# The low part of a weight block: one half by a VectorE subtraction, the other by an accumulating transfer

## The chip, the cores and the metric

The kernel runs on one core of a Trainium2 chip. The metric is the device time of one execution in microseconds (us); a lower one is better. The engines are named as in the profile: PE is TensorE's matrix products and PEld its weight loads, DVE is VectorE, ACT is ScalarE, POOL is GpSimd, SP is SyncE, which issues most of the transfers.

## What is computed

The reference runs a sequence of 512 tokens of width 1024 through three layers and computes everything in float32. The first layer has pooling beside latent attention, the second has differential attention, and each is followed by a gated feed-forward of width 2816. The third layer mixes three kinds of heads (a stick-breaking attention, a gated recurrence and an attention over 256 memory rows) and ends in a routed block: for each token and each of 8 heads, the 16 best of 16384 experts are chosen and weighted.

```python
def swiglu(h, w_gate, w_up, w_down):
    return (jax.nn.silu(h @ w_gate) * (h @ w_up)) @ w_down
...
h = rms_norm(x, norm_mix_gain[l])
proj = h @ w_in[l]
...
x = x + mixed @ w_out[l]
x = x + peer_ffn(rms_norm(x, norm_ffn_gain[l]), peer_w_query[l], ...)
```

## The kernel before, in words

Every product with a weight matrix is made in split form. A weight w is split into a high part, which is w rounded to the faster matrix type (FR in the code), and a low part, which is w minus the high part. The activations are split in the same way. A product is then three matrix products: high by high, high by low and low by high (`mm3`, L265 to L268; `tok_mm`, L278 to L286, is the same with the tokens as the stationary side, at L283 to L285).

`load_w` (L244) brings in one block of weights, mostly 256 columns of a 1024-row matrix, which is 128 x 2048 numbers or 1 MB. It does so in two halves of 128 x 1024. For each half SyncE loads the numbers into a `raw` buffer (L253), ScalarE copies them into `whi` with rounding (L228), and an engine given by the list LO subtracts `whi` from `raw` into `wlo` (L229). `raw`, `whi` and `wlo` have three buffers each (RB and WB, L32), which is one and a half blocks. With 256 tokens a block means 48 matrix products of 256 columns.

Which engine subtracts is set for a stretch of the program by `low(n)` (L240):

```python
LO = [V, V]
def low(n):
    LO[:] = [GP] * n + [V] * (2 - n)
```

So with n = 2 GpSimd makes both halves, with n = 1 GpSimd makes the first and VectorE the second, and with n = 0 VectorE makes both. The stretches are:

- LO_Q = 2 (set at L886): the second layer's attention, with its query, key and value projections and the first part of its output projection; 17 blocks. `low(0)` at L893 ends it.
- LO_A = 0 (L952): the second layer's feed-forward for the first 256 tokens (`ffn1(0)`).
- LO_Y = 2 (L1354): the memory's projections and the third layer's projections for the first 256 tokens (`memory`, `projections`), with the feed-forward of the other 256 tokens (`ffn_b`) begun beside them.
- LO_M = 2 (L1357): the mixer of the first half with `ffn_b` beside it, its output projection (`HA.output`), the norm, and the routing queries of that half (`PA.queries`) with `ffn_b` beside them. LO_Y and LO_M hold 56 blocks together.
- LO_Z = 1 (L1724): the rest of `ffn_b`, the projections of the second half, its mixer and its output projection; 22 blocks.
- LO_P = 1 (L1743): the queries of the second half and the expert scores; 72 blocks.

The order of the work has two sources. `alongside` and `side_by_side` (L152 to L182) interleave generators by given step counts, for example `alongside((mixer(HA), 200), (ffn_b, F_2))` at L1359. The order on each engine is then laid out at build time by the tile framework's planner (`schedule_with_timeline_sim=True`, L1799), which knows the dependences and its own estimates of durations; on the chip each engine runs its list in order. `tc.high_priority` draws the small steps of a reciprocal root forward (`rsqrt`, L288 to L300: eleven VectorE steps on a few columns, one after another).

GpSimd also makes some sums of squares (L366, L945), the masks and running sums of the stick-breaking attention (L1252, L1263, L1266), memsets, and it issues the gathers of expert rows (L1516), which are kept in program order. In the routing (`route` and `decode`, L1449 to L1512) VectorE finds the best 16 of the scores; its steps with two operands in SBUF are the candidate sums (L1479) and the one-hot products (L1501, L1504). On SyncE stand the weight loads, one behind another.

## Time and profile before

| what | value |
|---|---|
| median of 3 runs | 3099.04 us (3092.49 to 3104.55) |
| profiled execution | 3092.14 us |
| its span, first to last instruction | 3090.4 us |
| mean granted clock of TensorE | 0.977 |
| busy share: TensorE, its weight loads, VectorE, ScalarE, GpSimd | 95%, 82%, 70%, 44%, 38% |
| the chain that ended last: TensorE, VectorE, transfers | 71%, 18%, 5% |
| moved by SyncE's queue, by GpSimd's queue | 427.61 MB, 137.71 MB |

The table shows one execution in the small, and the runs in its first line. A busy share is an average over stages with different limits, so it says little about what one stage waits for; the views by stage do that. TensorE's products are pipelined: a product's own duration is longer than the time from one to the next. The granted clock is TensorE's, as a share of the full 2.4 GHz. An engine's idle time is counted in front of the instruction that ends it, with what released that instruction. The transfers that GpSimd issues are nearly all gathers of expert rows, and they begin, but for one, after 1800 us.

### The profile page before, as it was taken

What the parts mean: (1) busy time and instruction counts of PE and PEld (TensorE: products, weight loads), DVE (VectorE), ACT (ScalarE), POOL (GpSimd) and SP (SyncE); (2) the same over time, 40 slices, a digit from 0 to 9 for tenths busy, and PEclk for the clock granted to TensorE, in tenths of its full rate; (3) what the DMA queues carried; (4) which work ended last, traced back from release to release, by engine and by line L of the source; (5) the groups of instructions that cost most, each with busy time, mean ns of one, the idle gap of its engine ahead of it and who ended that gap; (6) DMA issues with size and microseconds to landing.
All of it is one profiled execution on the core that took longest, in us unless ns stands there. A gap on an engine that the chain in (4) does not pass through costs nothing.

```text
span 3090.4 us, 44585 instructions
## 1 busy us (share of the span) xinstructions
PE 2923.3 (95%) x16770; PEld 2539.4 (82%) x16770; DVE 2154.9 (70%) x3873; ACT 1370.7 (44%) x2347; POOL 1163.8 (38%) x722
## 2 busy tenths in 40 slices
PE   8999999999989979999879989889999999999999
PEld 6468888877679978789878588889999998777887
DVE  6755434477766755757986658999778758888753
ACT  4443222366544544554344543336656643333332
POOL 3110000243330177466654136555545535445200
PEclk9999999999999999999999989999999999999999
DMA  3012232321145534244443057777888789999964
GB/s 131 28 62 103 86 107 85 104 69 42 28 144 195 181 130 142 77 150 150 135 138 119 1 176 278 258 269 260 292 307 293 286 300 390 369 377 377 342 228 147
DMA packets 195881, 568.29 MB, mean 184 GB/s; under 512 B 16944, under 2 KB 68528, under 8 KB 194000
## 3 DMA queue, kind: packets, MB, share of 16 engines
q1 hardware_dynamic: 157664, 427.61, 40.1%
q0 software_dynamic: 37712, 137.71, 11.9%
q8 instruction: 132, 2.16, 0.3%
q14 instruction: 85, 0.70, 0.1%
q10 hardware_dynamic: 288, 0.11, 0.0%
HBM read 512.93 MB, written 52.43 MB: 183 GB/s over the span
## 4 chain that ended last, share of the span: by engine, by line
PE 71%; DVE 18%; DMA 5%; issue 3%; ACT 2%; POOL 1%; SPq 0%; DVEq 0%; ACTq 0%; POOLq 0%
PE ps L266 14%; PE ps L268 14%; PE ps L267 14%; PE ps L1682 4%; PE ps L1683 4%; PE ps L1681 4%; DVE wlo L229 2%; PE ps L1563 2%; DVE u L1530 2%; PE ps L482 2%; DMA u<-in_peer_v_dram,ix 1%; DMA u<-in_peer_u_dram,ix 1%; PE ps L475 1%; PE ps L283 1%; PE ps L285 1%
## 5 line engine op out<-in xcount | busy, mean ns | idle before, releaser
L229 POOL TENSOR_TENSOR wlo<-raw,whi 128x1024 fp32r<-128x1024 f32 (+2 forms) x240 | 595.7, 2490 | 584.8 <-ACT whi L228 571.0
L228 ACT ACTIVATE whi<-raw 128x1024 fp32r<-128x1024 f32 (+2 forms) x518 | 516.2, 998 | 644.3 <-PE ps L267 367.3
L229 DVE TENSOR_TENSOR wlo<-raw,whi 128x1024 fp32r<-128x1024 f32 (+3 forms) x278 | 351.0, 1264 | 215.3 <-ACT whi L228 214.6
L268 PE MATMUL ps<-yh,wlo 128*128 128x384 f32 (+1 forms) x1152 | 387.0, 337 | 29.4 <-DVE wlo L229 29.3
L266 PE MATMUL ps<-yh,whi 128*128 128x384 f32 (+1 forms) x1152 | 390.8, 339 | 0.0
L267 PE MATMUL ps<-yl,whi 128*128 128x384 f32 (+1 forms) x1152 | 385.4, 335 | 0.0
L1682 PE MATMUL ps<-vl,gh 128*128 128x512 f32 x768 | 300.6, 391 | 5.4 <-DVE vl L229 5.2
L1683 PE MATMUL ps<-vh,gl 128*128 128x512 f32 x768 | 299.3, 390 | 0.0
L266 PE MATMUL ps<-XH,whi 128*128 128x512 f32 (+1 forms) x680 | 273.1, 406 | 8.7 <-ACT whi L228 8.7
L1516 POOL DMA_INDIRECT u<-in_peer_v_dram,ix x128 | 203.2, 1587 | 195.6 <-DVE h L1595 174.2
L267 PE MATMUL ps<-XL,whi 128*128 128x512 f32 (+1 forms) x680 | 267.6, 396 | 0.0
L268 PE MATMUL ps<-XH,wlo 128*128 128x512 f32 (+1 forms) x680 | 263.0, 395 | 1.9 <-DVE wlo L229 1.9
L268 PEld LDWEIGHTS ps<-yh,wlo 128*128 128x128 f32 x1152 | 220.6, 192 | 34.3 <-DVE wlo L229 34.2
L1681 PE MATMUL ps<-vh,gh 128*128 128x512 f32 x768 | 239.5, 392 | 9.2 <-ACT vh L228 9.2
L228 ACT ACTIVATE vh<-raw 128x1024 fp32r<-128x1024 f32 x128 | 133.3, 1055 | 250.0 <-DMA raw<-in_peer_v_dram 174.4
L1530 DVE SCALAR_TENSOR_TENSOR u<-u,h 128x1024 f32<-128x1024 f32 x127 | 190.1, 1502 | 49.3 <-DMA u<-in_peer_u_dram,ix 49.3
L267 PEld LDWEIGHTS ps<-yl,whi 128*128 128x128 f32 x1152 | 221.0, 192 | 0.0
L266 PEld LDWEIGHTS ps<-yh,whi 128*128 128x128 f32 x1152 | 220.9, 192 | 0.0
L366 POOL TENSOR_TENSOR sqa<-sqa,sq 128x512 f32<-128x512 f32 (+1 forms) x28 | 40.8, 1456 | 450.3 <-ACT sq L364 449.4
L266 PE MATMUL ps<-fx,whi 128*128 128x256 f32 x704 | 199.2, 287 | 4.5 <-ACT whi L228 3.1
L268 PE MATMUL ps<-fx,wlo 128*128 128x256 f32 x704 | 193.9, 284 | 6.9 <-DVE wlo L229 4.6
L229 DVE TENSOR_TENSOR vl<-raw,vh 128x1024 fp32r<-128x1024 f32 x128 | 155.0, 1221 | 63.2 <-ACT vh L228 62.7
(427 smaller groups left out, 7146.8 us busy)
## 6 DMA issues: line engine op xcount, KB each, us to landing
raw<-in_uT_dram SPq DMA_DIRECT2D x128, 512.0 KB, 5.8
raw<-in_peer_v_dram SPq DMA_DIRECT2D x128, 512.0 KB, 7.0
raw<-in_w_gate_dram SPq DMA_DIRECT2D x66, 512.0 KB, 3.7
raw<-in_w_up_dram SPq DMA_DIRECT2D x66, 512.0 KB, 3.7
raw<-in_w_in_dram SPq DMA_DIRECT2D x52, 512.0 KB, 3.8
Sd<-s SPq DMA_DIRECT2D x32, 768.0 KB, 7.0
Gd<-st SPq DMA_DIRECT2D x12, 2048.0 KB, 10.4
gt<-Gd SPq DMA_DIRECT2D x32, 768.0 KB, 8.7
```

Source lines behind the costliest of these rows:

```text
L228: SC.activation(hi, src, AF.Copy)
L229: eng.tensor_sub(lo, src, hi.bitcast(F))
L266: PE.matmul(out, wh, xh, start=first, stop=False)
L267: PE.matmul(out, wh, xl, start=False, stop=False)
L268: PE.matmul(out, wl, xh, start=False, stop=last)
L482: PE.matmul(po[hd], vtile(hd, j), t[hd, j], start=j == 0, stop=j == nk - 1)
L1516: i = GP.indirect_dma_start(out=u, out_offset=None, in_=A[table], in_offset=bass.IndirectOffsetOnAxis(ap=self.idx[t, hd][:, j:j + 1], axis=0))
L1530: V.scalar_tensor_tensor(u, u, 1.0, self.h2[t], op0=OP.mult, op1=OP.mult, accum_out=self.sd[t][:, hd, j:j + 1])
L1563: PE.matmul(p[:, n * 128:(n + 1) * 128], q[:, n], e[:, n], start=True, stop=True)
L1681: PE.matmul(p, gh[:, e, ts], h[:, cs], start=False, stop=False, skip_group_check=True)
L1682: PE.matmul(p, gh[:, e, ts], l[:, cs], start=False, stop=False, skip_group_check=True)
L1683: PE.matmul(p, gl[:, e, ts], h[:, cs], start=False, stop=end, skip_group_check=True)
```

## The change

Where LO names the new marker ADDED for a half, the low part is no longer subtracted by an engine. ScalarE makes the high part as before, and then writes minus the high part into `wlo`. GpSimd then issues a transfer that reads the same weights from HBM once more and adds them to what stands in `wlo`. The half's `raw` buffer is needed for the high part alone.

`low(n, other)` now gives the first 2 - n halves to VectorE and the last n to `other`, which is GpSimd where nothing is said. So the order of the halves is turned wherever n = 1. LO_Q, LO_Y and LO_M go from 2 to 1, and with LO_Z (1 as before) they name ADDED: in these stretches VectorE subtracts the first half and a transfer makes the second. LO_P keeps n = 1 with GpSimd, but VectorE now has the first half and GpSimd the second. LO_A is as it was.

```diff
--- before.py
+++ after.py
@@ -31,7 +31,7 @@
 LOWEST = -3.0e38
 RB, WB = 3, 3
 U2, UZ, UD = 3, 3, 4
-LO_A, LO_Y, LO_M, LO_Z, LO_P = 0, 2, 2, 1, 1
+LO_A, LO_Y, LO_M, LO_Z, LO_P = 0, 1, 1, 1, 1
 VB = 4
 HI, HX = 100, 1
 K_S = 8
@@ -43,7 +43,7 @@
 V_0, D_0, N_0, T_0 = 1, 0, 2, 6
 PX, EVX, XX = 1, 0, 1
 Y_F = 0, 4, 0, 0
-LO_Q = 2
+LO_Q = 1
 AT = 2, 6
 E_B = 8, 3
 GB, SB = 1, 1
@@ -237,9 +237,11 @@
         MIXING = [False]
         LO = [V, V]
 
-        def low(n):
-
-            LO[:] = [GP] * n + [V] * (2 - n)
+        ADDED = object()
+
+        def low(n, other=GP):
+
+            LO[:] = [V] * (2 - n) + [other] * n
 
         def load_w(ap, kt, eng=LO):
 
@@ -253,7 +255,12 @@
                 nc.sync.dma_start(raw, ap[:, a * w:b * w])
                 hi = wp.tile([128, 1024], FR, name="whi", bufs=WB)[:, :c]
                 lo = wp.tile([128, 1024], FR, name="wlo", bufs=WB)[:, :c]
-                split(hi, lo, raw, eng[i])
+                if eng[i] is ADDED:
+                    SC.activation(hi, raw, AF.Copy)
+                    SC.activation(lo, hi.bitcast(F), AF.Copy, scale=-1.0)
+                    GP.dma_start(lo, ap[:, a * w:b * w], accum_op=OP.add)
+                else:
+                    split(hi, lo, raw, eng[i])
                 parts.append((hi, lo))
 
             def get(k):
@@ -883,7 +890,7 @@
                 assert scaled[-1] >= 6
                 yield from out_half(A["w_dout"], XH, XL, 1, held, N_0)
 
-            low(LO_Q)
+            low(LO_Q, ADDED)
             for _ in qk(0):
                 pass
             held, scaled = [], []
@@ -1351,10 +1358,10 @@
             yield from steps(h.items(), {H_B[0]: [lambda: between_roots(h.q0)], H_B[1]: [lambda: between_rows(h.q0)]})
             between_inner(h.q0)
 
-        low(LO_Y)
+        low(LO_Y, ADDED)
         alongside((chain(memory(), projections(HA)), 24), (ffn_b, F_1))
         open_mix()
-        low(LO_M)
+        low(LO_M, ADDED)
         MIXING[0] = True
         alongside((mixer(HA), 200), (ffn_b, F_2))
         MIXING[0] = False
@@ -1721,7 +1728,7 @@
 
         alongside((normed(0, W, xh, xl), 20), (ffn_b, F_3))
         alongside((PA.queries(), 112), (ffn_b, F_4), (gather_a, L_4))
-        low(LO_Z)
+        low(LO_Z, ADDED)
         for _ in ffn_b:
             pass
         HB = Half(W, big)
```

## Rows read from the trace of the kernel before

**Rows 1.** busy time, share of the span and instructions of each engine.
```profile
PE 2923.3 (95%) x16770; PEld 2539.4 (82%) x16770; DVE 2154.9 (70%) x3873; ACT 1370.7 (44%) x2347; POOL 1163.8 (38%) x722
```

**Rows 2.** by stage: us, busy us (instructions) per engine, granted clock, DMA share, GB/s.
```profile
607.00:890.00 283.00, 278.96 (x1318) 204.21 (x1318) 198.85 (x472) 160.18 (x310) 110.60 (x71) 0.99 0.20 65
1055.00:1200.00 145.00, 126.03 (x1030) 124.42 (x1028) 75.10 (x142) 71.53 (x115) 101.85 (x65) 0.95 0.45 150
1200.00:1345.00 145.00, 132.34 (x941) 116.34 (x937) 108.51 (x291) 73.20 (x129) 73.82 (x58) 0.94 0.26 90
1345.00:1400.00 55.00, 47.86 (x361) 45.97 (x362) 28.63 (x63) 24.60 (x42) 33.45 (x14) 0.88 0.45 152
1450.00:1595.00 145.00, 117.81 (x916) 113.80 (x915) 142.62 (x409) 58.51 (x98) 93.25 (x47) 0.93 0.43 141
1595.00:1670.00 75.00, 71.92 (x596) 70.88 (x595) 44.99 (x83) 36.37 (x51) 34.08 (x22) 0.97 0.51 174
1800.00:2100.00 300.00, 265.53 (x1584) 260.42 (x1585) 269.62 (x645) 107.48 (x181) 171.41 (x96) 0.94 0.71 247
```

**Rows 3.** groups by shape: busy us, mean ns; last row of 890 to 1055.
```profile
L229 POOL TENSOR_TENSOR wlo<-raw,whi 128x1024 fp32r<-128x1024 f32 x224 | 571.1, 2558 | 550.9 <-ACT whi L228 537.2 <-PE ps L1563 7.1 <-DVE wlo L229 5.7
...
L228 ACT ACTIVATE whi<-raw 128x1024 fp32r<-128x1024 f32 x428 | 451.5, 1056 | 495.9 <-PE ps L267 246.3 <-DMA raw<-in_uT_dram 66.9 <-issue 46.0
...
L229 DVE TENSOR_TENSOR wlo<-raw,whi 128x1024 fp32r<-128x1024 f32 x56 | 69.4, 1243 | 38.7 <-ACT whi L228 38.7
```

**Rows 4.** timeline from 1091.2 us: start us, us, engine, line, operation.
```profile
1091.28 2.38 POOL L229 TENSOR_TENSOR wlo<-raw,whi 128x1024 fp32r<-128x1024 f32 x1
1091.37 2.31 DVE L299 TENSOR_TENSOR rs_c<-rs_c,rs_y 128x2 f32<-128x2 f32 x1
...
1097.37 0.16 DVE L300 SCALAR_TENSOR_TENSOR rcol<-rs_c,rs_y 128x2 f32<-128x2 f32 x1
```

**Rows 5.** chain of waits, 1055 to 1200, then 1200 to 1345: start us, us.
```profile
1088.36 2.29 DVE rs_y L300
...
1125.44 2.22 DVE rs_c L298
...
1200.91 2.40 DVE hg_ks L1186
...
1295.45 2.36 DVE hg_qs L1182
```

**Rows 6.** VectorE groups of 1450 to 1595; then their lines, ns min/median/max.
```profile
L1479 DVE TENSOR_TENSOR cand<-ts 128x256 f32<-128x256 f32 x12 | 14.2, 1179 | 0.0
L1501 DVE TENSOR_TENSOR oh<-af,iota 128x1024 f32<-128x1024 f32 x8 | 13.1, 1642 | 0.0
...
L1499 DVE CAST af<-ai 128x64 f32<-128x64 int32 x8 | 10.0, 1250 | 0.0
...
L1479 DVE TENSOR_TENSOR cand<-ts x32: 398/809/2342, 1426.2 to 2083.9; 128x256 f32<-128x256 f32 x32
L1501 DVE TENSOR_TENSOR oh<-af,iota x16: 1198/1213/3405, 1478.4 to 2126.2; 128x1024 f32<-128x1024 f32 x16
L1499 DVE CAST af<-ai x16: 166/183/2390, 1475.6 to 2116.7; 128x64 f32<-128x64 int32 x16
```

**Rows 7.** GpSimd's plain loads: KB, us to landing; then one issue's ns.
```profile
m<-in_memT_dram POOLq DMA_DIRECT2D x1, 1024.0 KB, 8.8
...
mraw<-in_masks_dram POOLq DMA_DIRECT2D x1, 512.0 KB, 5.9
...
L1007 POOL DMA_DIRECT2D mraw<-in_masks_dram x1: 536/536/536, 871.2 to 871.2; - x1
```

**Rows 8.** busy us and instructions on low parts (wlo), 1450 to 1595.
```profile
1450.00:1595.00 145.00, 80.18 (x288) 55.00 (x287) 9.36 (x7) 78.62 (x32) 0.93 0.43 141
```

**Rows 9.** TensorE's waits, 1055 to 1600, then 1800 to 2100: us, times, longest.
```profile
PE ps L268 <- POOL wlo L229: 7.8, 7, 1.9
...
PE ps L268 <- DVE wlo L229: 29.3, 18, 3.6
```

## The prediction

> **What bounds the kernel now.** I read the page's busy times first [rows 1]: TensorE is busy 95% of the span, so only time in which it stands idle, or runs at the lower clock, can be won. Then the busy times by stage [rows 2], where the reader sees that the idle time is not spread evenly. In the stage of the memory and first projections (1055 to 1200 us) TensorE is busy 126.0 of 145 us, in the first mixer 132.3 of 145, in its output and the norm after it 47.9 of 55, in the query stage (1450 to 1595) 117.8 of 145: 19.0, 12.7, 7.1 and 27.2 us idle. In the query stage VectorE is busy 142.6 of 145 us, so there VectorE is the bound. In the second half's queries (1800 to 2100) TensorE idles 34.5 us.
>
> Next I asked what makes VectorE late. The groups by shape [rows 3] show that a subtraction of 128x1024 takes 2558 ns on GpSimd and 1243 on VectorE where GpSimd makes none. The timeline [rows 4] shows them against each other: a VectorE step on two columns, 0.16 us when alone, took 2.31 us, and it ended with the GpSimd subtraction that had begun 0.09 us before it. The chain of waits [rows 5] passes through seven such pieces in the projection stage (first and last shown, 1.88 to 2.32 us, 15.5 us in all) and nine in the first mixer. In the query stage the same shapes hold VectorE [rows 6]: the candidate sum takes 1179 ns in the mean and 398 at least, the index cast 1250 against 166, the one-hot 1642 against 1198.
>
> **The change, part by part.** From the code: 17 loads of weights are made under LO_Q, 56 under LO_Y and LO_M, 22 under LO_Z, 72 under LO_P; each has two halves.
>
> Removed: GpSimd's subtractions, 34 under LO_Q, 112 under LO_Y and LO_M and 22 under LO_Z, 168 of the 240 on the page; 72 under LO_P stay. The GpSimd time itself is worth nothing (38% busy); what counts is that VectorE is no longer held.
> - Projection stage: seven pieces, 15.5 us, less 7 x 0.16 of their own: 14 us, on a path for which TensorE waits, and under its 19.0 us of idle. I take -14. Ends: 0, if the subtractions that VectorE takes over stand in the same places; -19, all the idle time.
> - First mixer and its output: nine pieces of 1.8 us or more, some 20 us over their own time, but idle is 12.7 + 7.1, and VectorE takes 20 subtractions more (40 halves were GpSimd's, half of them) at 1.2 us, 24 us, in a stage in which it is busy 108.5 of 145. I take -9. Ends: +4 and -20.
> - Query stage: 12 x (1179 - 398) + 8 x (1250 - 166) + 8 x (1642 - 1198) = 9.4 + 8.7 + 3.6 = 21.7 us that VectorE gets back. It pays: 39 halves are made here, 32 by GpSimd and 7 by VectorE [rows 8]; afterwards VectorE has 19.5, so 12.5 more at 1.2, 15 us. That alone leaves -7; other steps with two operands are held too, and I put them at a further -6: -13, since VectorE is the bound here. Ends: +15 and -27 (TensorE's idle).
> - Clock: the granted clock is 0.93 to 0.95 in the three long stages and 0.88 in the output, worth 7, 9, 10 and 7 us; it falls where TensorE has stood idle. With less than half of the idle gone I take -7; ends 0 and -15.
>
> Added on ScalarE: 95 copies that make minus the high part, 1056 ns each by the like-shaped copy [rows 3], 0.1 ms over some 1000 us in which ScalarE is about half busy [rows 2]. They lie beside TensorE; what waits behind one is the next half's high part and the evacuations. Cost 0, within +10; below nothing is excluded, as ScalarE gives no work away.
>
> Added on GpSimd's queue: 95 issues. A plain issue there occupies it 0.54 us [rows 7]; each now waits for the ScalarE copy as the subtraction waited for the high part. Behind it stand the mixer's masks and sums (L1252, L1263, L1266) and, at the very start of the last part, one gather; they had 2.4 us in front of them and now have 0.5. Cost 0, ends -2 and +5.
>
> Added latency, the dear part: after its buffer is free, a second half was ready after a high part and a GpSimd subtraction, 1.06 + 2.4 = 3.5 us. Now it takes 1.06 + 1.06 + 0.54 + the landing. The nearest row is the plain GpSimd load of 512 KB: 5.9 us to landing; the one of 1024 KB took 8.8 [rows 7]. So 8.6 us (11.5 if an accumulation moves twice the bytes), 5.1 us more. Three buffers hold one and a half loads. A load is 48 matrix products at 75 us / 596, 0.126 us: 6.0 us where nothing else runs (36 loads: 2 + 13 + 4 + 13 + 4), and over 8 us where the feed-forward interleaves. A buffer serves one half in 1.5 loads, 9.0 us, so 8.6 us fits, if TensorE's order puts the products with the low part late, and does not if they stay where they are. At present TensorE waits for a GpSimd low part 7 times, 7.8 us, in the stages from 1055 to 1600 [rows 9]. I take 0.4 us for each of the 36 dense loads: +14. Ends: 0 (order adapted) and 36 x 5.1 = +184.
> By the Trainium skill, "DMA: Bandwidth & Descriptors", section "Anatomy of one DMA — SWDGE (gpsimd) path", such a transfer takes about 2.0 us plus its bytes at 436 GB/s, an estimate of 3.2 us for 512 KB. The row measured 5.9, and the sum goes by the row; by the page the second half would be 2.4 us later than now, not 5.1, and the +14 would be about +7.
>
> Attention under LO_Q (607 to 890): TensorE idles 4 of 283 us [rows 2], GpSimd loses 34 subtractions, VectorE gains 17; ±0, ends -4 and +15, covered by TensorE's own work.
>
> Order turned under LO_P: the second half goes to GpSimd, the first to VectorE. Now TensorE waits 29.3 us for VectorE's halves [rows 9], which are the second ones; afterwards those have half a load more time, but GpSimd's get that much less and share its queue with the gathers. VectorE's sum does not change. 0, ends -29 and +29. LO_Z turns as well, at 0 by the same reasoning.
>
> Transfers: SyncE issues as before; a raw buffer of a DMA-made half comes free after the high part, 2.4 us sooner. Nothing is late for it now: 0.
>
> Sum: -14 - 9 - 13 - 7 + 14 = -29. The profiled execution took 3092.1 us (span 3090.4), so 3063; the median of the runs shown is 7 above it, so I forecast 3070.
>
> **The rivals.**
> 1. Second halves late, slower. Place: TensorE's products with the second half's low part in the 36 dense loads. If the order is laid out for a shorter transfer than the chip's, each such load stalls; as a stall also gives the next transfer time, half of the 5.1 us stays: 36 x 2.5 = 92 in place of my 14, so 3070 + 78 = 3148, and 3117 with two loads of three. It decides above 1.2 us a load, where the gain of 43 is gone. For it: three buffers only, and a chain of four steps on three engines. Against: each build lays TensorE's order out anew, and can put the products with a late low part last. Chance 0.25.
> 2. The DMA engines fill. In the second projections they are busy 0.51 at 174 GB/s [rows 2]. Half a load more makes 0.77; if accumulated bytes are moved twice, 1.02, and the 36 loads run at the transfers' pace, at least 0.02 x 6.0 us longer each, with raw loads landing later by what a busy queue shows. I price it at 1 us a load: 36 in place of 14, 3092. Chance 0.08. The Trainium skill, "DMA: Bandwidth & Descriptors", section "Rules for kernel authors", says that an accumulating transfer reads its destination and writes it later; no row here shows one.
> 3. No gain: VectorE's own 73 extra subtractions (73 x 1.2 = 88 us) fill the places that GpSimd's blocking leaves, and the time of before stays: 3099, within 8. For it: VectorE is full in the query stage. Chance 0.17.
> 4. The turned order under LO_P frees TensorE as well: 29 us off my sum, 3041. Chance 0.10.
> My forecast itself (3050 to 3083): 0.40.
>
> **How the numbers follow.** A difference of 0.5%, 15.5 us, is about what this measurement can tell from none: faster means under 3083.5, slower over 3114.5. Faster is my case, most of it, and rival 4, with a little of rival 2: 0.50. Slower is rival 1 but for its mild end, and a little of 2 and 3: 0.29. The rest is 0.21. Gains reach to 3025 (rival 4 with the far ends of the query stage and the clock), losses to 3150, rival 1 at its full price. My own case's range is 3050 to 3083.
>
> **What would show it.** Right: the two-column steps back at 0.2 us in 1055 to 1200, VectorE under 135 us of the query stage with the candidate sum near 400 ns, no GpSimd subtraction before the last part. Wrong: TensorE's waits for a low part from a DMA over 50 us in all, its idle time in the second projections (now 3.1 us of 75) grown, landings of the accumulating transfers over 9 us, or the waits of 1800 to 2100 doubled.

## The result, and the profile after

The changed kernel takes 3192.3 us (median of 4 runs, 3176.7 to 3203.4) against 3098.8 for the kernel before on the same chip: a ratio of 1.0306, 95% interval 1.0285 to 1.0328. It is slower by 3%. The forecast was 3070 us, with a range from 3025 to 3150. The profiled execution took 3186.6 us, its span 3184.8.

The busy times of the changed kernel, in the order of [rows 1]:

```profile
PE 2962.5 (93%) x16770; PEld 2569.3 (81%) x16770; DVE 2070.0 (65%) x3946; ACT 1464.5 (46%) x2442; POOL 840.2 (26%) x649
```

VectorE is 85 us less busy and GpSimd 324 us, although VectorE makes 73 subtractions more. So VectorE is held far less. The query stage shows it. Here are the changed kernel's VectorE groups there (1465 to 1640 us), for [rows 6]:

```profile
L1508 DVE TENSOR_TENSOR oh<-af,iota 128x1024 f32<-128x1024 f32 x7 | 8.5, 1215 | 0.0
...
L1486 DVE TENSOR_TENSOR cand<-ts 128x256 f32<-128x256 f32 x14 | 5.9, 420 | 0.0
...
L1506 DVE CAST af<-ai 128x64 f32<-128x64 int32 x8 | 2.1, 264 | 0.0
```

The candidate sum takes 420 ns in place of 1179, the one-hot 1215 in place of 1642, the index cast 264 in place of 1250. The Trainium skill, "SBUF — State Buffer", section "Who interferes with whom", says that a VectorE operation with two inputs in SBUF and a GpSimd operation that reads SBUF share a port, and that the second to issue stands still; [rows 4], the candidate sum and the one-hot agree. The cast has one input, so that sentence doesn't cover it, but the rows show that it was held as well.

What took its place stands in TensorE's waits of the changed kernel, 1055 to 1900 us (us in total, times, longest). L275 and L291 are the products with the low part:

```profile
PE ps L275 <- DMA wlo<-in_w_in_dram: 25.9, 16, 4.8
PE ps L275 <- DMA wlo<-in_w_query_dram: 15.6, 7, 3.7
...
PE ps L275 <- DMA wlo<-in_w_down_dram: 14.0, 7, 3.9
PE ps L275 <- DMA wlo<-in_w_out_dram: 10.9, 4, 3.6
PE ps L275 <- DMA wlo<-in_w_up_dram: 10.2, 6, 3.2
PE ps L275 <- DMA wlo<-in_w_gate_dram: 9.5, 5, 2.6
PE ps L291 <- DMA wlo<-in_w_in_dram: 7.1, 5, 2.2
...
PE ps L275 <- DMA wlo<-in_w_mem_dram: 1.0, 1, 1.0
```

The reader is to see one releaser in all of them: an accumulating transfer. They come to 94.2 us in 51 waits. The kernel before had 7.8 us for GpSimd's low parts [rows 9] and one wait more at its other product:

```profile
PE ps L284 <- POOL wlo L229: 1.7, 1, 1.7
```

One of the waits for a transfer, in the changed kernel's chain of waits (start us, us):

```profile
1165.98 1.07 ACT whi L259
1167.08 1.07 ACT wlo L260
1168.15 0.28 issue
1168.44 7.34 DMA wlo<-in_w_in_dram
1175.82 0.38 PE ps L291
```

From the high part's start to the product that needs the low part it is 9.8 us; the prediction had 8.6. The piece of 7.34 us runs from the start of the transfer's issue. The issue itself is longer too. The changed kernel's instructions of line 261 (ns: least, median, most):

```profile
L261 POOL DMA_DIRECT2D wlo<-in_w_in_dram x26: 856/865/942, 1104.2 to 1713.8; - x26
```

**Where the time went, by stage.** The stages are taken from SyncE's first issue of one weight to that of the next (us, one profiled execution each); the 576 to 578 us ahead of the first w_qkv are left out. The two columns on the right are of experiment 4 and of the first version of experiment 10.

| stage | before | after | plain transfer | both halves on VectorE |
|---|---|---|---|---|
| attention and its feed-forward (first w_qkv to first w_mem) | 495.1 | 499.8 | 490.7 | 498.5 |
| memory and first projections (to last w_in of the first half) | 106.7 | 110.9 | 103.4 | 94.2 |
| first mixer and output (to first w_query) | 201.5 | 214.1 | 185.2 | 184.2 |
| query stage (to first w_in of the second half) | 185.1 | 204.7 | 177.7 | 168.9 |
| second projections (to last w_in) | 84.9 | 99.1 | 91.9 | 87.3 |
| second mixer and output (to first uT) | 137.8 | 153.3 | 151.7 | 148.6 |
| routing (to first peer_v) | 729.8 | 750.3 | 746.1 | 726.4 |
| the rest | 571.9 | 576.2 | 576.5 | 572.9 |

The five stages from w_mem to uT, here called the dense stages, lose 66 us (716.0 to 782.1), the routing stage 20, which has one accumulating transfer, at its very start. In the dense stages TensorE is idle more and also busy longer, at a lower granted clock. The kernel before, then the changed one, from w_mem to uT (us, busy us and instructions of PE, PEld, DVE, ACT, POOL; clock, share of the transfer engines, GB/s):

```profile
1073.00:1789.00 716.00, 637.05 (x4698) 576.03 (x4697) 504.41 (x1355) 336.52 (x582) 401.51 (x257) 0.95 0.35 118
```

```profile
1076.00:1858.00 782.00, 657.93 (x4676) 588.80 (x4674) 454.40 (x1409) 411.35 (x658) 141.03 (x200) 0.93 0.62 159
```

So 45 of the 66 us are idle time and 21 are longer busy time.

### The profile page after: what moved, and what is told of

It is laid out like the page before. It is cut to its first block, busy times and chain, and to the rows that moved or that the text cites. A ratio compares the mean times of both kernels' runs of the same rounds, so it can differ in the third digit from the quotient of the medians.

```text
span 3184.8 us, 44722 instructions
## 1 busy us (share of the span) xinstructions
PE 2962.5 (93%) x16770; PEld 2569.3 (81%) x16770; DVE 2070.0 (65%) x3946; ACT 1464.5 (46%) x2442; POOL 840.2 (26%) x649
## 3 DMA queue, kind: packets, MB, share of 16 engines
q0 software_dynamic: 51392, 185.43, 20.2%
## 4 chain that ended last, share of the span: by engine, by line
PE 60%; DMA 14%; issue 12%; DVE 10%; ACT 3%; POOL 2%; SPq 0%; POOLq 0%; DVEq 0%; ACTq 0%
PE ps L275 12%; PE ps L273 12%; PE ps L274 12%; DMA u<-in_peer_u_dram,ix 4%; PE ps L1689 4%; PE ps L1690 4%; PE ps L1688 4%; DMA wlo<-in_w_in_dram 2%; PE ps L1570 2%; PE ps L489 2%; DMA raw<-in_peer_v_dram 2%; DVE wlo L229 2%; DMA wlo<-in_w_down_dram 1%; DVE u L1537 1%; PE ps L482 1%
## 5 line engine op out<-in xcount | busy, mean ns | idle before, releaser
L228 ACT ACTIVATE whi<-raw 128x1024 fp32r<-128x1024 f32 (+2 forms) x423 | 420.0, 993 | 537.3 <-PE ps L274 401.7
L229 DVE TENSOR_TENSOR wlo<-raw,whi 128x1024 fp32r<-128x1024 f32 (+2 forms) x351 | 419.3, 1196 | 256.9 <-ACT whi L228 245.5
L275 PE MATMUL ps<-yh,wlo 128*128 128x384 f32 (+1 forms) x1152 | 387.4, 338 | 22.5 <-DVE wlo L229 20.2
L229 POOL TENSOR_TENSOR wlo<-raw,whi 128x1024 fp32r<-128x1024 f32 x72 | 187.2, 2600 | 334.9 <-ACT whi L228 297.4
L1537 DVE SCALAR_TENSOR_TENSOR u<-u,h 128x1024 f32<-128x1024 f32 x127 | 188.1, 1489 | 131.8 <-DMA u<-in_peer_u_dram,ix 131.6
L275 PE MATMUL ps<-XH,wlo 128*128 128x512 f32 (+1 forms) x680 | 262.9, 396 | 3.4 <-DVE wlo L229 1.8
L275 PEld LDWEIGHTS ps<-yh,wlo 128*128 128x128 f32 x1152 | 221.5, 193 | 25.8 <-DVE wlo L229 23.1
L275 PE MATMUL ps<-xh,wlo 128*128 128x256 f32 x576 | 166.5, 305 | 52.4 <-DMA wlo<-in_w_in_dram 25.9
L275 PE MATMUL ps<-fx,wlo 128*128 128x256 f32 x704 | 196.6, 290 | 19.8 <-DMA wlo<-in_w_up_dram 10.2
L273 PE MATMUL ps<-fx,whi 128*128 128x256 f32 x704 | 200.9, 290 | 3.7 <-ACT fx L357 3.7
L274 PE MATMUL ps<-fx,whi 128*128 128x256 f32 x704 | 199.0, 287 | 0.9 <-DVE fx L358 0.9
```

Of the source, the lines that this page charges most:

```text
L228: SC.activation(hi, src, AF.Copy)
L229: eng.tensor_sub(lo, src, hi.bitcast(F))
L273: PE.matmul(out, wh, xh, start=first, stop=False)
L274: PE.matmul(out, wh, xl, start=False, stop=False)
L275: PE.matmul(out, wl, xh, start=False, stop=last)
L1537: V.scalar_tensor_tensor(u, u, 1.0, self.h2[t], op0=OP.mult, op1=OP.mult, accum_out=self.sd[t][:, hd, j:j + 1])
```

## The experiments

All times are medians of several runs; a ratio is to the kernel before on the same chip.

**1. The turned order of the last part, taken back.** In the changed kernel:

```
-        low(LO_P)
+        LO[:] = [GP, V]
```

> The changed kernel with one thing undone: in the last part (low(LO_P)) GpSimd makes the first half of a block and VectorE the second again, as before the change. In the changed kernel's profile the stretch from the second half's queries to the end of the routing (2070 to 2608 us) takes some 23 us more than before the change, and the stages under accumulating transfers some 70 us. Theory A (two causes: second halves late where the transfer makes them, and the turned order in the last part): 3192 - 23 = 3169 us, and the lag behind the kernel before stays at about 70 us from the start of the last part on. Rival B (the turned order is worth nothing; the 23 us come from what the earlier stages leave late): 3192 us, within 8. TensorE's waits for VectorE's low parts in that stretch, 20.2 us in the changed kernel: about 29 us by both, as before the change, since the order is the old one; so those waits don't decide it, the time does.

3174.5 us, ratio 1.0252 (1.0226 to 1.0277), against 1.0306: 17 us back. Its routing stage takes 721.9 us in place of 750.3; that is 28 us, but the profiled execution is the shortest of the five. Theory A.

**2. The turned order alone.** In the kernel before:

```
-        low(LO_P)
+        LO[:] = [V, GP]
```

> The kernel before with one thing done: in the last part VectorE makes the first half of a block and GpSimd the second. No accumulating transfer. Theory A: 3099 + 23 = 3122 us, all of the loss after 2070 us. Rival B (the turned order is worth nothing by itself): 3099 us, within 8. Rival C (it frees TensorE from the 29 us of waits for VectorE's second halves, as one case of the prediction had it): 3070 us.

3111.1 us, ratio 1.0045 (1.0028 to 1.0062): 14 us slower, with the routing stage at 745.5 in place of 729.8. That is between rival B (3099, within 8) and theory A (3122), nearer to A; C is out. VectorE's waits in that stage name the path. First the kernel before (1795 to 2545 us), then this one:

```profile
DVE u L1530 <- DMA u<-in_peer_u_dram,ix: 49.3, 30, 6.7
```

```profile
DVE u L1530 <- DMA u<-in_peer_u_dram,ix: 131.3, 40, 8.7
```

The rows u are gathered by transfers that GpSimd issues, in program order. With GpSimd on the second half its subtractions wait longer, for the high part and for a buffer that TensorE frees, and the gathers stand behind them on GpSimd's queue. GpSimd's waits in the kernel before and in this one, 1795 to 2545 us:

```profile
POOL wlo L229 <- ACT whi L228: 270.0, 59, 8.7
...
POOL wlo L229 <- PE ps L1563: 7.1, 2, 5.6
```

```profile
POOL wlo L229 <- ACT whi L228: 290.2, 55, 19.6
POOL wlo L229 <- PE ps L1563: 29.9, 3, 12.1
```

Laid over each other in the trace, 100 of VectorE's 131 us of waits for u fall while GpSimd waits for a low part's inputs or makes it; in the kernel before it is 36 of 49. What VectorE makes too late then holds TensorE at the small products of the routing (L1563), here in the kernel before and in this one:

```profile
PE ps L1563 <- ACT oe L1576: 1.3, 4, 0.8
```

```profile
PE ps L1563 <- ACT oe L1576: 13.9, 7, 2.9
```

The changed kernel shows the same 131.6 us of waits for u, experiment 1 shows 44.0.

**3. One half on VectorE, no transfer.** In the kernel before:

```
-LO_A, LO_Y, LO_M, LO_Z, LO_P = 0, 2, 2, 1, 1
+LO_A, LO_Y, LO_M, LO_Z, LO_P = 0, 1, 1, 1, 1
...
-LO_Q = 2
+LO_Q = 1
```

> The kernel before with its counts alone changed: under LO_Q, LO_Y and LO_M GpSimd subtracts one half of each block (the first) and VectorE the other, so GpSimd makes 73 subtractions fewer and VectorE 73 more; no accumulating transfer. This is the relief of VectorE from half of GpSimd's blocking without any transfer. Theory A (the relief is real, the transfers took it back): the terms of the prediction without its transfers would give 3099 - 43 = 3056 us if all of GpSimd's blocking went; with half of it left, some 3075 us. Rival B (VectorE's extra 73 x 1.2 = 88 us fill what the blocking leaves): 3099 us, within 10. Rival C (VectorE becomes the bound in the query stage, where it is busy 142.6 of 145 us): 3110 to 3125 us.

3074.0 us, ratio 0.9927 (0.9904 to 0.9950). Theory A: the relief is real, and the 73 subtractions that VectorE gains don't eat it.

**4. A plain transfer in place of the accumulating one.** This kernel leaves out the addition, so the low parts made so are whole weights and its time alone is of use.

```
-                    GP.dma_start(lo, ap[:, a * w:b * w], accum_op=OP.add)
+                    GP.dma_start(lo, ap[:, a * w:b * w])
```

> The changed kernel with a plain transfer in place of the accumulating one: it writes the weights over the low part and doesn't add to it, so the low parts of those halves are not the low parts; everything else, the two copies on ScalarE, the order and the count of transfers, stays. In the changed kernel an accumulating transfer of 512 KB is 6.8 us from issue to last packet and takes about twice the transfer engines' time of a plain one. Theory A (the stalls come from the length of the path, two copies, the issue and a start of some 1.6 us, which a plain one has as well): landing some 5 to 5.9 us, 1 to 2 us less for each of 36 dense loads, so at most about half of the 70 us comes back: 3150 to 3185 us. Rival B (the accumulation's double traffic fills the transfer engines): their share in the dense stretches falls from 0.73 to 0.81 to some 0.6 and nearly all of the 70 us comes back: 3122 to 3130 us.

3100.4 us, ratio 1.0015: 92 us back, more than either theory allowed. The instructions of every engine stand in the same order in both kernels, so the difference is the transfer's alone. In the dense stages it takes 710 us in place of 782. Of these 72 us 49 are idle time of TensorE, as much as its waits for these transfers fall (44.4 us from 92.7), and 23 are busy time: the clock is 0.96 in place of 0.93 (the lines stand in the first section and in experiment 9). Nor does GpSimd's longer issue cost by way of GpSimd's other steps: TensorE waits for those 4.8 us in the changed kernel and 5.2 in this one. The lines for line 261 here (the last one: least, median, most):

```profile
L261 POOL DMA_DIRECT2D wlo<-in_w_in_dram x26: 527/527/607, 1093.5 to 1633.2; - x26
...
DMA to landing us min/median/max: 3.2/5.2/8.0
```

and the software queue's share of the transfer engines (packets, MB, share), in the changed kernel and in this one:

```profile
q0 software_dynamic: 51392, 185.43, 20.2%
```

```profile
q0 software_dynamic: 51392, 185.43, 16.9%
```

The issue is 0.34 us shorter. From the records of the packets in the dense stages: a 4 KB packet takes 366 ns when it accumulates and 202 plainly (means), and the last of the 128 packets of a half ends 6.8 us after the start of the issue (median), plainly 5.0. Open was what costs the 92 us: that each transfer is longer, or that the transfer engines as a whole are too full.

**5, 6, 7. More lead, a shorter path.** One more buffer for low parts (and one in place of two for three scratch tiles of the mixers, sq, xp, hn_b); minus the high part straight from the raw block; both together.

```
-                lo = wp.tile([128, 1024], FR, name="wlo", bufs=WB)[:, :c]
+                lo = wp.tile([128, 1024], FR, name="wlo", bufs=WB + 1)[:, :c]
...
```

> The changed kernel with four buffers for low parts in place of three; so that they fit, three small scratch tiles of the mixers (sq, xp, hn_b) have one buffer in place of two, which may cost the mixers something. The plain transfer in place of the accumulating one gave back 92 us, with the same order of instructions on every engine; a transfer's last packet ends 4.8 us after its issue begins in place of 6.8. Theory A (the transfer's own length is what TensorE waits for; its path has to fit into the lead that the buffers give): a fourth buffer gives half a load more of lead, some 3 us, more than the 2.0 us by which the transfer is too long, so TensorE's waits for transfers between 1055 and 1900 us, 94 us, fall under 40, and the time to 3110 to 3140 us. Rival B (the transfer engines are too full, at a share of 0.73 to 0.81 in the dense stretches): more lead doesn't help, 3180 to 3200 us, and the waits stay at 80 or over.

```
-                    SC.activation(hi, raw, AF.Copy)
-                    SC.activation(lo, hi.bitcast(F), AF.Copy, scale=-1.0)
+                    SC.activation(lo, raw, AF.Copy, scale=-1.0)
+                    SC.activation(hi, raw, AF.Copy)
```

> The changed kernel with ScalarE making minus the high part straight from the raw block, ahead of the high part itself (the same rounding, with the scale at -1), so that the accumulating transfer can be issued one copy (1.06 us) earlier after its raw block has landed; same number of copies and transfers. Theory A (the length of the path from a free buffer to the landed low part): the plain transfer took 2.0 us off that path and gave back 92 us, 46 us for each us of path, so 1.06 us give back some 49: 3143 us. The high part comes 1.06 us later, which may take some 10 of it. Rival B (the transfer engines are too full): 3192 us, within 10.

> The changed kernel with four buffers for low parts (and one in place of two for sq, xp and hn_b) and minus the high part made from the raw block ahead of the high part. With four buffers alone ScalarE still waited 87 us, 55 times, for TensorE to free a buffer of high parts before it could start the path, so the lead had not grown; here the path doesn't pass through the high part's buffer any more, so the fourth buffer is lead. Theory A (length of the path against the lead): some 3 us more of lead than the 2 us that the transfer is too long; TensorE's waits for transfers between 1055 and 1900 us fall under 50 from 94, and the time to 3120 to 3150 us. Rival B (the transfer engines are too full): 3190 to 3210 us, waits of 80 or over.

The buffer alone: 3190.3 us, ratio 1.0316. The copy alone: 3207.7, ratio 1.0364 (1.0337 to 1.0392). Both: 3150.6, ratio 1.0166 (1.0145 to 1.0187). The first two missed theory A, and the third came at the end of its range (3120 to 3150), with 67.5 us of waits for transfers where it said under 50. Why the buffer alone didn't help stands in ScalarE's waits (1055 to 1900 us), of the changed kernel and of the one with four low buffers:

```profile
ACT whi L259 <- PE ps L274: 81.2, 51, 10.1
```

```profile
ACT whi L259 <- PE ps L274: 87.4, 55, 10.5
```

The path begins with the high part, and that still has three buffers; the lead, the work that TensorE has between a transfer's issue and its first use, had not grown. Why the copy alone is slower wasn't shown. With both, the path starts at the raw block, and 42 us come back.

**8. Less traffic.** Half of the raw columns where a transfer makes the low part, used twice; the accumulating transfer brings the whole half, so high and low part still add up to the weight, other than the expectation says.

```
+                if eng[i] is ADDED:
+                    raw = raw[:, :c // 2]
+                    nc.sync.dma_start(raw, ap[:, a * w:a * w + c // 2])
+                    raw = raw[:, None].to_broadcast([128, 2, c // 2])
...
```

> The changed kernel with less traffic beside the accumulating transfers: where a transfer makes the low part, only half of the columns of the raw block are loaded, and ScalarE makes the high part from those twice over (the same size of copy); so the products with those halves use wrong weights. The accumulating transfers themselves are as they were. By the traces a 4 KB packet takes about 200 ns plainly and 366 ns when it accumulates, so 128 packets cost the 16 engines 1.6 and 2.9 us: accumulating costs 1.3 us more of them for each half, and this edit takes 0.8 us back. Theory A (what TensorE waits for is the length of the transfer, 6.8 us from issue to last packet): 3180 to 3195 us. Rival B (the transfer engines are too full): 0.8 of 1.3 of the 92 us that the plain transfer gave back, so some 3135 us.

3197.4 us, ratio 1.0317 (1.0289 to 1.0345). The share of the transfer engines in the dense stages falls to 0.56 from 0.62, and no time comes back: against filled engines.

**9. The traffic without the length.** First with copies from DRAM to DRAM, issued by SyncE, in the kernel with plain transfers:

```
+                if eng[i] is ADDED:
+                    nc.sync.dma_start(spare.tile([128, 1024], F, name="spare", bufs=16)[:, :c], ap[:, a * w:b * w])
```

> The kernel with plain transfers (3100 us; the low parts of those halves are not low parts) with the traffic put back and not the length: for each of the 95 halves SyncE also issues a copy of the same 512 KB from DRAM to a spare place in DRAM, for which nothing waits. That gives the 16 engines some 1.6 us more for each half, about what accumulating costs over plain (1.3 us). Theory A (the length of the transfer): 3100 to 3120 us, the transfers a little longer by the traffic. Rival B (the transfer engines are too full): 3180 us or more.

3211.0 us, over rival B's 3180, and yet it tells nothing of the question. The stretch of 50 to 100 us, in this kernel and in the one with plain transfers (busy us of PE, PEld, DVE, ACT, POOL; clock, share, GB/s):

```profile
50.00:100.00 50.00, 21.14 (x80) 15.78 (x80) 17.31 (x47) 8.69 (x14) 5.77 (x6) 0.67 1.01 334
```

```profile
50.00:100.00 50.00, 44.17 (x173) 31.34 (x172) 40.70 (x76) 18.77 (x38) 18.61 (x15) 0.94 0.20 64
```

The copies waited for nothing and were all issued at the start, where they held the first weights back; from w_mem on the two kernels take 2027 and 2033 us. Then with stores that hang on the high part, with plain and with accumulating transfers:

```
+                    nc.scalar.dma_start(spare.tile([128, 1024], F, name="spare", bufs=16)[:, :c], hi.bitcast(F))
```

> The kernel with plain transfers (3100 us; the low parts of those halves are not low parts) with the traffic put back beside them in every stage: for each of the 95 halves ScalarE also issues a store of the high part, 512 KB, to a spare place in DRAM, for which nothing waits (the copies from DRAM to DRAM of the run before depended on nothing, were all issued in the first 200 us, and so said nothing of the dense stretches). Some 1.6 us more of the 16 engines for each half, about what accumulating costs over plain (1.3 us), with the plain transfer's length. Theory A (the length of the transfer): 3100 to 3120 us, and the share of the transfer engines in the dense stretches rises from 0.65 to some 0.8 all the same. Rival B (the transfer engines are too full): 3180 us or more.

> The changed kernel, accumulating transfers and all, with the stores of the high parts to a spare place in DRAM added: more traffic than the changed kernel, nothing taken away. With the stores TensorE's order had some 7.2 us of its own work between the issue of a transfer and the first product that needs it, in the median from 1085 to 1600 us, where the changed kernel has some 5.7 (by the traces, with plain transfers; the order of instructions is the same with accumulating ones). Theory A (a transfer costs what its length exceeds the work that the order puts in front of its first use): the stores lengthen the transfers by about 1.4 us, as they did the plain ones (4.9 to 6.3 us), and the order gives 1.5 us more, so it comes out near the changed kernel, 3165 to 3195 us, in spite of 48 MB more traffic. Rival B (the transfer engines are too full): clearly slower than the changed kernel, 3230 us or more, as their share would pass 0.9 in the dense stretches.

Plain and stores: 3104.7 us, ratio 1.0024 (1.0009 to 1.0039). Accumulating and stores: 3160.4, ratio 1.0221 (1.0186 to 1.0256): the changed kernel with 48 MB more traffic is 32 us faster than without, and a little faster than theory A said (3165 to 3195). The dense stages of four kernels (columns as above): the changed one stands in the first section (782 us, share 0.62); here are plain, plain and stores, accumulating and stores.

```profile
1067.00:1777.00 710.00, 634.97 (x4677) 568.13 (x4677) 450.64 (x1409) 409.96 (x659) 114.77 (x200) 0.96 0.54 175
```

```profile
1078.00:1774.00 696.00, 631.73 (x4692) 566.99 (x4691) 456.68 (x1410) 409.38 (x657) 119.76 (x200) 0.97 0.69 235
```

```profile
1071.00:1824.00 753.00, 644.78 (x4686) 576.93 (x4685) 460.27 (x1410) 409.91 (x659) 140.72 (x200) 0.95 0.75 217
```

The fastest of the four has fuller engines (0.69) than the slowest (0.62). So fuller engines as such don't order these kernels, and rival B is out. What orders them is the length against the lead. The lead is worked out from the traces: TensorE's busy time between the issue of a transfer and the first product with its low part. The length is from the issue to the last packet. Both are medians of the 77 or 78 transfers in the dense stages. The shortfall adds up, over these transfers, what the length is over the lead. The waits are TensorE's for these transfers.

| kernel | lead, us | length, us | shortfall, us | waits, us | dense stages, us |
|---|---|---|---|---|---|
| changed | 5.8 | 6.8 | 83 | 92.7 | 782 |
| plain transfer (same order) | 5.4 | 5.0 | 35 | 44.4 | 710 |
| four low buffers | 5.7 | 6.6 | 83 | 94.3 | 795 |
| minus from raw | 6.5 | 7.3 | 78 | 103.4 | 802 |
| both of these | 6.6 | 6.7 | 46 | 65.1 | 742 |
| half raw | 5.4 | 6.5 | 96 | 105.2 | 794 |
| plain and stores | 6.8 | 6.2 | 23 | 28.0 | 696 |
| accumulating and stores | 7.0 | 7.3 | 65 | 75.6 | 752 |

Where the lead is longer than the length the waits are 28 to 44 us, where it is shorter 65 to 105, and the shortfall comes within 5 to 25 us of the waits. The last two kernels have one order of instructions, as the changed and the plain one have. The stores helped because with them the order that was laid out has more TensorE work ahead of the first use.

**10. Versions without transfers, and a mild use of them.** Both halves on VectorE everywhere ahead of the last part; the second half on GpSimd; attention as the latter and the rest as the former; that one with accumulating transfers in attention alone; and with the old order for the second half's projections. All have the last part's old order.

```
LO_Q, LO_Y, LO_M, LO_Z:  0, 0, 0, 0
                         1, 1, 1, 1        (1 is [V, GP])
                         1, 0, 0, 0        (1 is [V, GP])
                         1, 0, 0, 0        (1 is [V, ADDED])
                         1, 0, 0, [GP, V]  (1 is [V, GP])
```

> No accumulating transfer and no GpSimd subtraction of weights ahead of the last part: VectorE makes both halves under LO_Q, LO_Y, LO_M and LO_Z; the last part as before the change (GpSimd first half, VectorE second). Theory A (what counts is that VectorE is held by GpSimd, and one half on VectorE, 3074 us, removed half of that): the rest goes too and the time falls further, to some 3060 us. Rival C (VectorE itself is the bound in the query stage: without GpSimd it needs 142.6 - 21.7 - 8 for the stage's other work, 113, and 39 x 1.2 = 47 for the subtractions, 160 us in a stage of 145): 3090 to 3115 us, with VectorE busy over 0.95 of the query stage.

> As the kernel with one half on VectorE (3074 us), but with the halves turned ahead of the last part: VectorE makes the first half and GpSimd the second under LO_Q, LO_Y, LO_M and LO_Z; the last part keeps the order of before the change. It tells what the turned order is worth in the stages ahead of the last part, which the changed kernel has too. Theory A (the order costs where GpSimd's slower half comes second and has no lead; it cost 14 us in the last part alone): 3085 us. Rival B (no matter there): 3074 us, within 6.

> A version meant to be faster, no transfers: under LO_Q GpSimd makes the second half of a block and VectorE the first, under LO_Y, LO_M and LO_Z VectorE makes both, the last part in the order of before the change. The kernel with both halves on VectorE everywhere ahead of the last part took 3059 us and reached the memory's weights at 1074 us; the one with GpSimd on the second half took 3062 us and reached them at 1071. If the stages add up: 3055 us. If attention's order doesn't matter: 3059 us, within 5.

> The fastest version so far (3048 us: attention's second halves on GpSimd, all others ahead of the last part on VectorE) with the accumulating transfer in attention alone, where a load of weights is needed only every 8 us or more and the transfer has time. It tells whether the transfer is harmless where loads are far apart. Theory A (length against lead): 3045 to 3055 us, the memory's weights reached within 5 us of 1070. Rival (the transfer costs wherever it stands, by GpSimd's longer issue or by its traffic): 3060 us or more.

> The fastest version so far (3048 us) with the second half's projections and output (LO_Z) made as before the change too: GpSimd first half, VectorE second, in place of both on VectorE. In the kernel with both halves on VectorE the second half's mixer and output took 148.6 us (from its last load of projections to the first of the routing), in the kernel before 137.8. If that is the subtractions' doing: some 11 us less, 3037 us. If those 11 us only move from one stage to the next (query stage to routing took 404.8 us in all there and 407.8 before): 3048 us, within 8.

| version | us | ratio | 95% |
|---|---|---|---|
| both halves on VectorE | 3059.2 | 0.9880 | 0.9853 to 0.9907 |
| second half on GpSimd | 3062.1 | 0.9903 | 0.9882 to 0.9924 |
| second half on GpSimd in attention alone | 3047.8 | 0.9853 | 0.9823 to 0.9884 |
| accumulating in attention alone | 3056.7 | 0.9866 | 0.9838 to 0.9895 |
| old order in the second half | 3052.6 | 0.9862 | 0.9838 to 0.9886 |

The first came out as its theory A had it, the third at 7 us under the sum of its stages. The last three can't be told apart; in the fifth the second mixer and output is 8 us shorter than in the third and the second projections 8 us longer, so the time only moves. The transfer does little harm in attention: the time is just above what theory A expected (3045 to 3055), and w_mem comes at 1074 us in place of 1070, in an execution at the slower of the two paces of the last section. The 11 transfers of 512 KB there are 6.0 us long and the 6 of 256 KB 4.2 (medians); the lead is 7.4 us in the median, the shortfall of all 17 comes to 0.2 us and TensorE's waits for them to 0.9. Ahead of the last part the turned order is a gain: 3062 against 3074 in experiment 3 (3058 to 3068 and 3072 to 3083), the other way round than it was expected, and than in the last part; why wasn't shown. VectorE alone fills the query stage and it is still the faster way; the version with both halves on VectorE, 1400 to 1520 us:

```profile
1400.00:1520.00 120.00, 115.61 (x954) 113.61 (x953) 120.00 (x390) 52.08 (x80) 0.00 (x0) 0.97 0.50 165
```

VectorE is busy all of the 120 us, and TensorE still 96% of them. From w_mem to uT TensorE's waits for VectorE's low parts come to 5.3 us, and it is idle 52 us of 684:

```profile
1074.00:1758.00 684.00, 632.27 (x4696) 569.84 (x4695) 533.33 (x1490) 338.90 (x582) 80.79 (x123) 0.95 0.37 123
```

## Why the prediction was wrong

- **Relief of VectorE: right.** The steps went back to about their own length, and the versions without transfers got the time: the kernel with both halves on VectorE is 12.5 us shorter in the projections (predicted 14), 17 in the first mixer and output (9), 16 in the query stage (13). It gives 13 back in the second projections and mixer, which the prediction had at nothing.
- **Added latency: the step that failed.** "I take 0.4 us for each of the 36 dense loads: +14." Against the kernel with both halves on VectorE the changed one takes 782.1 - 683.2 = 99 us more in the dense stages. By the lines of the two (first section and experiment 10) it is 72 us of idle time and 26 us of longer busy time, at a clock of 0.93 in place of 0.95. Three parts of the step were off.
  - Which loads: the 36 (w_mem, w_in, w_out) had 43.4 us of waits for transfers, 1.2 us each in place of 0.4. The other 42 of these stages (w_query and the feed-forward's), which the step left out since the feed-forward interleaves there, had 49.3 us, 1.2 us each as well, in place of nothing.
  - The path: 9.8 us in the chain, not 8.6. The issue takes 0.87 us, not 0.54, and what follows up to the product some 6.5. The 8.6 also has the issue twice, as the 5.9 us of [rows 7] run from its start; by those rows the path is 8.0 us, 4.5 more than before.
  - The order: "8.6 us fits, if TensorE's order puts the products with the low part late". It doesn't put them late. A plain and an accumulating transfer get the same order, so the layout didn't tell them apart, and a lead of 5.4 to 5.8 us suits the plain one (5.0 us) and not the accumulating one (6.8).
- **Rival 1 was the case**, and the prediction's own sign of it came (waits for a low part from a transfer over 50 us). Its price (2.5 us on each of 36 loads, 92 us) is near the 99 by luck: it is about 1.3 us on each of 78 loads. What spoke against it, that "each build lays TensorE's order out anew", was the wrong argument, as experiment 4 shows. Of the 44 us from its 3148 to 3192 the turned order takes some 17; the rest wasn't split.
- **Turned order under LO_P: 0 predicted, +14 and +17 measured** (experiments 2 and 1), inside the ends of 29 on either side. The sentence that GpSimd's halves "share its queue with the gathers" had the cause; TensorE's waits for VectorE's low parts did fall, to 20.2 us from 29.3, as the step said, and the gathers' lateness outweighed that.
- **Clock: -7 predicted, a loss found.** The granted clock of the dense stages is 0.95 before and 0.93 in the changed kernel, where TensorE stood idle 124 us in place of 79. It is 0.95 with both halves on VectorE too, so the relief alone didn't raise it either.
- **Rival 2, filled engines:** its bound (accumulated bytes cost twice) was near the mark, 366 ns a packet against 202, but full engines aren't what costs the time: experiments 8 and 9.
- **The range:** its low end, 3025, is 3019 by the terms that it names (3041 less 14 and 8).
- **The terms at 0:** the copies on ScalarE weren't tried by themselves. TensorE's waits for ScalarE's high parts are 1.3 us in the changed kernel's dense stages, so no cost is seen there. Experiment 4 has the like for GpSimd's queue.
- **By the page:** the Trainium skill, "DMA: Bandwidth & Descriptors", section "Anatomy of one DMA — SWDGE (gpsimd) path", gives about 2.0 us and the bytes at 436 GB/s, an estimate of 3.2 us for 512 KB. That is too short for both kinds here: in the dense stages a plain one landed after 5.4 us (median, 3.6 at least; the 3.2 of the line in experiment 4 is one of 256 KB), and the last packet of an accumulating one ended after 6.8. So the measurement decides.

## What to carry to other kernels

A step that moves from an engine to a transfer is paid for by its length against the work that the order puts in front of its first use; neither the transfer engines' share nor the engine time that was freed tells that. Find out first what order is laid out: here it was the order of a shorter transfer, and the uses waited, some 1.3 us on each of 78 loads, with what the lower clock cost. And before work is moved to a transfer, try it on the engine that is to be relieved: VectorE was held more by GpSimd than by its own work, and doing more of it itself made the kernel 1.2 to 1.5% faster.

## What was not expected

- The same code on TensorE runs at two paces, by execution. In 950 to 1030 us, with no wait and no accumulating transfer, TensorE is busy throughout at a granted clock of 1.00, in the changed kernel and in the one with plain transfers:

```profile
950.00:1030.00 80.00, 80.00 (x681) 80.00 (x681) 49.82 (x73) 35.02 (x45) 0.00 (x0) 1.00 0.54 185
```

```profile
950.00:1030.00 80.00, 80.00 (x709) 80.00 (x708) 51.41 (x76) 36.88 (x47) 0.00 (x0) 1.00 0.58 196
```

  One product starts every 118 ns in the former and every 113 ns in the latter. Both values turn up with and without the change (the kernel before has 113, experiments 2 and 3 have 118), so it doesn't come from the change. The attention stage takes 497.6 to 502.0 us in the six profiled executions at 118 ns and 490.7 to 498.5 in the eleven at 113 (experiment 9's first kernel, which starts late, left out), so the pace can account for its 4.7 us in the table. It doesn't account for the dense stages, since experiment 1 runs at 113 and takes 788 us there. What sets it stays open.
- Work for the transfer engines that waits for nothing is all issued at the start of the program: TensorE stood still 118.5 us for its first weights behind the copies of experiment 9, and 8.7 us in the kernel with plain transfers.
